# Odd mixer: the output product of six heads inside the last head pair, alpha x in pieces, DVE steps with a PSUM operand

## The chip, the core and the metric

One core of a Trainium2 chip runs the whole kernel, a two-layer diffusion backbone in float32. Five engines with their own instruction queues work on it: TensorE (PE: matmuls and transposes), VectorE (DVE), ScalarE (ACT), GpSimd (POOL), and SyncE (SP), which issues most DMAs. Each queue is worked off in order; an instruction that waits for another engine holds everything behind it on its own engine. The metric is device time in microseconds (us), as the median of several runs.

## What is computed

The part of the reference that the change touches is the odd layer's mixer and the layer norm behind it:

```python
def odd_mixer(h, hc, w_qkv, lam_p, subln_w, w_out, rot, lambda_init, need_ctx):
    ...                                  # q, k, v of 8 heads, rotary on q and k
    k_all = jnp.concatenate([kl, kc], axis=3)      # 512 latent + 256 context tokens
    ob = lax.map(lambda qq: diff_mix(qq, k_all, v_all, lam), qb)
    ...
    def finish(o):
        o = rms_norm(o) * subln_w.astype(f32) * (1.0 - lambda_init)
        return (merge_heads(o).astype(w_out.dtype) @ w_out).astype(h.dtype)

def diff_mix(q, k, v, lam):
    s = jnp.einsum('cbhqd,cbhkd->cbhqk', q, k).astype(jnp.float32) * DIFF_HD ** -0.5
    p = jax.nn.softmax(s, -1)
    a = p[0] - lam * p[1]
    return jnp.einsum('bhqk,bhkd->bhqd', a.astype(v.dtype), v)

x = layer_norm(DEEP_ALPHA * x + g_a * y, ln_g[li, 0], ln_b[li, 0])
hf = modulate(x, sh_f, sc_f)             # input of the FFN
```

The output product is 512 x 1024 by 1024 x 1024: 8 heads of 128 rows, 4 tiles of 128 tokens, and two halves of 512 columns.

## The kernel before

**Numbers in two parts.** Every float32 operand of a large product is split into a high and a low part, and a product is three matmuls (high by high, low by high, high by low). A weight unit is 1024 rows by 256 columns: `unit` (L174) loads it over SP into one of two `raw` buffers (1 MB), GpSimd multiplies it by a gate row where one is given (L185), ACT casts the high part `whi` (L147), and GpSimd or DVE subtracts to get `wlo` (L148). The next load into a `raw` buffer waits until its `wlo` is made.

**Head pairs.** `odd_mixer` works on four pairs of heads. While `attend` works on pair `pr`, head by head and tile by tile, `project(pr + 1)` is put in between step by step: matmuls `opj`, then the rotary steps on DVE (L1576, L1580) with their last sum `otok` on GpSimd (L1582), PE's transposes `oT_ps` of it, and evacuations into `oq` and `ok` on ACT and DVE (L1590 to L1601). A scheduler orders the instructions of each engine by priority.

**One tile of attention.** PE makes the scores `sc`; DVE takes two maxima (L1662), ACT two exponentials (L1665), DVE combines them into `pt` (L1673); PE transposes `pt` into `aT_ps`, ACT and DVE copy it to `aT` (L1681), PE multiplies by v, DVE copies the result into `oall` (L1685), ACT sums its squares (L1686). After four tiles of a head, DVE computes the reciprocal root on 128x4 tiles (`rsqrt`, L127 to L136) and scales `oall` by it and by the subln weight, four steps with two SBUF operands (L1695).

**Output product.** `to_y(h)` transposes a head of `oall` (`yT_ps`) and splits it into `hTh` and `hTl` (L1704, L1705). In the last pair, which has no projection to put in, `sums` fills in the product of heads 0 to 5 for tiles 0 and 1 and the first half of the columns, at a late priority. The rest of the product runs after attention. Units 0 and 1 have no gate; their half of the result is multiplied by the gate on DVE (L1345). Units 2 and 3 are multiplied by the gate on GpSimd. `out_proj_ln` (L1299) then reads x of the layer before, makes alpha x (the normalization's affine part times alpha: product L1323 on DVE, sum L1324 on GpSimd), adds the product (L1346, L1348), normalizes, and makes the FFN's transposed input; the FFN's first matmul is `g_ps`.

Of the kernel before, what the change touches and what calls it, by code (L numbers as in the profile page):

```python
# [97 lines left out]
class Net:  # L98
# [21 lines left out]

    def rsqrt(self, pool, x, n, mul, add, tag):
# [52 lines left out]
    def unit(self, parts, scale=None):  # L174
# [1113 lines left out]
    def out_part(self, accs, units, k, last):  # L1288

        yh, yl = self.hT  # L1290
        for t, ps in accs:
            ts = slice(t * P, (t + 1) * P)
            for u, (wh, wl) in enumerate(units):
                for j, (xi, wi) in enumerate(((yh, wh), (yh, wl), (yl, wh))):
                    self.mm(ps[:, u * 256:(u + 1) * 256], xi[:, k, ts], wi[:, k, :],
                            start=(k == 0 and u == 0 and j == 0), stop=(last and u == 1 and j == 2))

    def out_proj_ln(self, l, w_out, key, src, xh, groups, accp, accs, us, trp, gates=None):

        nc = self.nc  # L1300
        with ExitStack() as st:
            lnp = self.pool(st, f"lnA{l}")
            pp = accp if l == 0 else self.pool(st, f"ps_wout{l}", bufs=2, space=PSUM)
            self.ln_pools(st, f"lnA{l}", trp=trp)
            self.lo_engs = "v"
            self.cparts = 2
            if l == 0:
                self.wps = [self.pool(st, f"wout{l}", bufs=2, side="right")]
                us = [us, [self.unit([w_out[:, u * 256:(u + 1) * 256]]) for u in (2, 3)]]
            if l == 0:  # L1310
                gates = self.gate_rows(lnp, l, 0, 2, self.ln2.tile([P, D], F32, tag="gy", bufs=3, name="gy"))
            else:

                lng, lnb = self.affine_rows(lnp, 0, 1)
                for r in (lng, lnb):
                    nc.scalar.activation(r, r, AF.Copy, scale=ALPHA)

            def load_x(tiles):
                for t in tiles:
                    lx[t] = self.ln2.tile([P, D], F32, tag="lx", bufs=4 if l else 2, name="lx")  # L1320
                    nc.sync.dma_start(out=lx[t], in_=self.x_src(src, t))
                    if l:
                        nc.vector.tensor_mul(lx[t], lx[t], lng)  # L1323
                        nc.gpsimd.tensor_add(lx[t], lx[t], lnb)  # L1324

            lx = {}
            if l:
                load_x((0, 1, 2, 3))
            for grp in groups:
                if l == 0:  # L1330
                    load_x(grp)
# [207 lines left out]
    def odd_mixer(self, acc_st):  # L1539
        nc, a = self.nc, self.a  # L1540
        v, g, s_ = nc.vector, nc.gpsimd, nc.scalar
        with ExitStack() as st0:
            y = self.hT
            pj = self.pool(st0, "ps_opj", bufs=2, space=PSUM)
            with ExitStack() as st:
# [161 lines left out]
                def sums(accs, heads, late=0):  # L1707
                    for h in heads:
                        to_y(h)
                        with self.priority(late):  # L1710
                            self.out_part(accs, us[0], h, h == DHEADS - 1)
# [99 lines left out]
```

## Time and profile before

| what | value |
|---|---|
| median of 3 runs | 2072.14 us (2070.14 to 2078.73) |
| the profiled execution | 2068.32 us |
| its span | 2066.5 us |
| its mean granted TensorE clock | 0.979 |
| PE busy | 1939.9 us (94%) |
| DVE busy | 1231.5 us (60%) |
| GpSimd busy | 775.6 us (38%) |
| ACT busy | 716.3 us (35%) |

The odd mixer takes about 1262 to 1674 us of the span, its last head pair about 1570 to 1628. A busy PE share is counted with matmuls that overlap one another in the pipeline; the distance between the starts of two matmuls in a row is their true price. In square brackets behind a row stands the engine's idle time before it and what ended that time.

### The profile page before, as it was taken

Reading aid. Unit: us, or ns where it says so; the run is one execution under the profiler, and the core shown is the slowest. Engines: PE = TensorE matmul, PEld = TensorE weight load, DVE = VectorE, ACT = ScalarE, POOL = GpSimd, SP = SyncE. Lnnn points to the kernel's source line nnn. Section 1 sums busy time; section 2 is a strip of 40 time slices with the busy share of each in tenths; the row PEclk is TensorE's granted clock in tenths of the full one; section 3 lists DMA queues with packets and bytes.
Section 4 is the critical chain, followed back from the end, with each engine's and each line's share of the span. In section 5 each row is a group of like instructions: output and inputs, shape, how many; then the busy total and the mean of one; then the engine's idle time right before and its main releaser. Section 6 shows DMA issues by size and latency. Waiting matters only on the chain. (4 is left out here: it accounts for less than half of the span.)

```text
span 2066.5 us, 33438 instructions
## 1 busy us (share of the span) xinstructions
PE 1939.9 (94%) x13766; PEld 1666.0 (81%) x13766; DVE 1231.5 (60%) x2423; ACT 716.3 (35%) x1252; POOL 775.6 (38%) x412
## 2 busy tenths in 40 slices
PE   6999999999899999999999998999997989999997
PEld 4777777778888888888888887989896987888886
DVE  2344745444367686666666557356667687756667
ACT  3341343423343432222222225454555343323221
POOL 1233323212322154554554434122213126756572
PEclk8999999999999999999999999999999999999999
DMA  8456344455614321111111112011103143323221
GB/s 261 140 166 178 110 134 141 127 168 169 201 49 156 102 82 62 62 62 62 62 62 62 62 62 90 22 42 42 42 32 95 59 143 102 93 91 102 82 82 41
DMA packets 195585, 201.33 MB, mean 97 GB/s; under 512 B 21112, under 2 KB 183512, under 8 KB 195432
## 3 DMA queue, kind: packets, MB, share of 16 engines
q1 hardware_dynamic: 194136, 197.57, 30.7%
q8 instruction: 108, 1.77, 0.3%
q10 hardware_dynamic: 1296, 1.62, 0.2%
q14 instruction: 45, 0.37, 0.1%
HBM read 185.89 MB, written 13.27 MB: 96 GB/s over the span
## 5 line engine op out<-in xcount | busy, mean ns | idle before, releaser
L148 POOL TENSOR_TENSOR wlo<-raw,whi 128x2048 fp32r<-128x2048 f32 (+2 forms) x154 | 413.6, 2709 | 483.0 <-ACT whi L147 459.7
L1441 DVE SCALAR_TENSOR_TENSOR ac<-g_ps,fconvT,ac 128x441 f32<-128x441 f32 (+2 forms) x352 | 243.8, 694 | 189.0 <-ACT ac L1430 179.3
L147 ACT CAST whi<-raw 128x2048 fp32r<-128x2048 f32 (+2 forms) x177 | 200.3, 1169 | 379.9 <-PE d_ps L115 163.3
L115 PE MATMUL d_ps<-whi,hh 128*128 128x512 f32 x440 | 176.2, 401 | 11.4 <-DVE gt L1390 6.5
L115 PE MATMUL d_ps<-whi,hl 128*128 128x512 f32 x440 | 173.5, 394 | 0.6 <-DVE hl L148 0.6
L115 PE MATMUL d_ps<-wlo,hh 128*128 128x512 f32 x440 | 173.1, 393 | 0.0
L115 PE MATMUL opj<-whi,hTh 128*128 128x256 f32 x512 | 148.1, 289 | 2.1 <-ACT oq L1593 1.6
L115 PE MATMUL g_ps<-hTl,whi 128*128 128x512 f32 (+1 forms) x384 | 145.1, 378 | 3.2 <-POOL hTl L148 3.2
L115 PE MATMUL opj<-whi,hTl 128*128 128x256 f32 x512 | 146.7, 287 | 0.0
L115 PE MATMUL opj<-wlo,hTh 128*128 128x256 f32 x512 | 145.6, 284 | 0.0
L115 PE MATMUL u_ps<-hTh,whi 128*128 128x512 f32 (+1 forms) x384 | 144.6, 377 | 0.0
L115 PE MATMUL u_ps<-hTh,wlo 128*128 128x512 f32 (+1 forms) x384 | 144.6, 377 | 0.0
L115 PE MATMUL g_ps<-hTh,whi 128*128 128x512 f32 (+1 forms) x384 | 144.6, 377 | 0.0
L115 PE MATMUL u_ps<-hTl,whi 128*128 128x512 f32 (+1 forms) x384 | 144.5, 376 | 0.0
L115 PE MATMUL g_ps<-hTh,wlo 128*128 128x512 f32 (+1 forms) x384 | 144.2, 376 | 0.0
L115 PE MATMUL fpj<-whi,hTh 128*128 128x256 f32 x432 | 125.9, 291 | 0.9 <-ACT fo L683 0.9
L115 PE MATMUL fpj<-wlo,hTh 128*128 128x256 f32 x432 | 125.8, 291 | 0.0
L115 PE MATMUL fpj<-whi,hTl 128*128 128x256 f32 x432 | 124.6, 288 | 0.0
L115 PEld LDWEIGHTS d_ps<-whi,hh 128*128 128x128 f32 x440 | 83.3, 189 | 38.9 <-DVE gt L1390 17.2
L115 PEld LDWEIGHTS opj<-whi,hTh 128*128 128x128 f32 x512 | 98.4, 192 | 4.2 <-ACT oq L1593 2.6
L115 PE MATMUL c_ps<-hTh,wlo 128*128 128x256 f32 x352 | 98.9, 281 | 0.0
L115 PE MATMUL c_ps<-hTh,whi 128*128 128x256 f32 x352 | 98.8, 281 | 0.0
(459 smaller groups left out, 4985.2 us busy)
## 6 DMA issues: line engine op xcount, KB each, us to landing
mraw<-in_mod_w_dram SPq DMA_DIRECT2D x80, 512.0 KB
raw<-in_f_w_gate_dram SPq DMA_DIRECT2D x22, 1024.0 KB
raw<-in_f_w_up_dram SPq DMA_DIRECT2D x22, 1024.0 KB
raw<-in_f_w_down_dram SPq DMA_DIRECT2D x22, 1024.0 KB
raw<-in_o_w_qkv_dram SPq DMA_DIRECT2D x12, 1024.0 KB
raw<-in_e_w_in_dram SPq DMA_DIRECT2D x10, 1024.0 KB
mraw<-in_mod_w_dram SPq DMA_DIRECT2D x32, 256.0 KB
raw<-in_e_w_in_dram SPq DMA_DIRECT2D x12, 512.0 KB
```

What stands on the lines that cost most here:

```text
L115: self.nc.tensor.matmul(out, lhsT=lhsT, rhs=rhs, start=start, stop=stop)
L147: self.nc.scalar.copy(h, r)
L148: lo_eng.tensor_sub(l, r, h.bitcast(F32))
L1441: v.scalar_tensor_tensor(out=o, in0=pv[:, r0 + di:r1 + di, c0 + dj:c1 + dj], scalar=cw[(di + 1) * 3 + dj + 1], in1=o, op0=ALU.mult, op1=AL ...
```

## The change

- **Output product.** `early` replaces `sums`: heads 0 to 5 for all four tiles and both halves of the columns (288 matmuls) are filled into the last pair at the late priority, and DVE adds each PSUM result onto alpha x (`rest`). After attention there are heads 6 and 7 (96 matmuls), added by DVE from PSUM, then the normalization in place in `oall`.
- **Weights.** All four units take the gate on GpSimd, and before it a new ACT step multiplies the raw unit by the subln weight, one factor for each partition (`rows`). All four `wlo` are on GpSimd. Unit 0 is loaded in the third pair, unit 1 too in the order that the scheduler makes. The gate comes in two halves (`half_gate`), the first in the third pair.
- **Alpha x.** In the first two pairs `alpha_x(i)` makes alpha x of all rows in 16 pieces of 64 columns: SP reads the piece `xa` (rows of 256 B) and two rows `gb` of the affine part, ACT multiplies `gb` by alpha, GpSimd multiplies and adds (128x256 each), SP writes the piece to `xd[2]`. There is one `xa` and one `gb`. In the last pair the result is read back into `oall` and `rest`.
- **DVE.** `rsqrt_ps` holds y and the sum's addend `zz` in PSUM, so that each step has at most one SBUF operand; the four scalings of `oall` go to ACT.
- `out_proj_ln` now serves layer 0 alone, with the same work as before.

```diff
-    def unit(self, parts, scale=None):
+    def unit(self, parts, scale=None, rows=None):
...
+        if rows is not None:
+            nc.scalar.activation(raw, raw, AF.Copy, scale=rows)
         if scale is not None:
             nc.gpsimd.tensor_mul(rv, rv, scale.unsqueeze(1).to_broadcast([P, KT, 256]))
...
+    def rsqrt_ps(self, pool, hv, y, n, tag):
...
+        v.tensor_scalar(out=y.bitcast(I32), in0=hv.bitcast(I32), scalar1=-0.5, scalar2=MAGIC,
+                        op0=ALU.mult, op1=ALU.add)
+        for i in range(3):
+            v.tensor_mul(w, y, hv)
+            v.tensor_mul(w, y, w)
+            v.scalar_tensor_tensor(out=r if i == 2 else y, in0=w, scalar=1.5, in1=y, op0=ALU.subtract, op1=ALU.mult)
+        return r
...
-                    zz = pb.tile([P, NLT], F32, tag="orz", name="orz")
-                    s_.activation(zz, Zs[:, :, 0], AF.Square, scale=math.sqrt(2 * DH * NORM_EPS))
-                    v.tensor_add(ss, ss, zz)
-                    r = self.rsqrt(pb, ss, NLT, 1.0 / (2 * DH), 0.0, "on")
+                    zz, yy = (ps[:, 3 * P + i * NLT:3 * P + (i + 1) * NLT] for i in range(2))
...
+                    r = self.rsqrt_ps(pb, ss, yy, NLT, "on")
                     for t in range(NLT):
-                        v.scalar_tensor_tensor(out=oall[:, t, hc], in0=oall[:, t, hc], scalar=r[:, t:t + 1], in1=sub,
-                                               op0=ALU.mult, op1=ALU.mult)
+                        s_.activation(oall[:, t, hc], oall[:, t, hc], AF.Copy, scale=r[:, t:t + 1])
...
+                def early(heads):
+
+                    for n in range(2):
+                        for t in range(NLT):
+                            ps = pj.tile([P, 512], F32, tag="wo", name="wo_ps")
+                            with self.priority(LATE):
+                                for h in heads:
+                                    self.out_part([(t, ps)], us[n], h, h == heads[-1])
+                                    if h == heads[len(heads) // 2 - 1]:
+                                        yield
+                                for o, c0, n_ in rest(t, n):
+                                    v.tensor_add(o, ps[:, c0:c0 + n_], o)
+                            yield
...
+                def out_unit():
+                    sl = slice(len(us) * 256, (len(us) + 1) * 256)
+                    us.append(self.unit([w_out[:, sl]], gates[len(us) // 2][:, (len(us) % 2) * 256:][:, :256],
+                                        sub[:, 0:1]))
...
+                def alpha_x(i):
+
+                    cs = slice(i * 64, (i + 1) * 64)
+                    nc.sync.dma_start(out=xa, in_=self.xd[1][:LAT, cs].rearrange("(t p) n -> p t n", p=P))
+                    for j, n in enumerate(("ln_g", "ln_b")):
+                        nc.sync.dma_start(out=gb[:, j], in_=a[n][0, 1, cs].partition_broadcast(P))
+                    s_.activation(gb, gb, AF.Copy, scale=ALPHA)
+                    for j, op in enumerate((g.tensor_mul, g.tensor_add)):
+                        op(xa, xa, gb[:, j].unsqueeze(1).to_broadcast([P, NLT, 64]))
+                    nc.sync.dma_start(out=self.xd[2][:LAT, cs].rearrange("(t p) n -> p t n", p=P), in_=xa)
...
                         for _ in attend(2 * pr + i, cur["q"], cur["k"], cur["v"], i):
                             with self.priority(100 if pr < 3 else 0):
-                                for _ in range(3 if pr < 3 else 1):
+                                for _ in range(3 if pr < 3 else 2):
                                     next(fill, None)
+                            done += 1
+                            if pr < 2:
+                                alpha_x(8 * pr + done - 1)
+                            if pr == 2 and done == 6:
+                                out_unit()
                     for _ in fill:
                         pass
+                for h in (6, 7):
+                    to_y(h)
```

How the change moves instructions, at three places.

GpSimd, first head pair, around the rotary sums `otok` of the second pair's k and q. Before:

```order
L1582 TENSOR_TENSOR otok_12500<-otok_12500,ob_12501 128x512
L1582 TENSOR_TENSOR otok_12564<-otok_12564,ob_12565 128x512
L1582 TENSOR_TENSOR otok_12738<-otok_12738,ob_12739 128x512
L1582 TENSOR_TENSOR otok_12802<-otok_12802,ob_12803 128x512
L148 TENSOR_TENSOR wlo_13197<-raw_13194,whi_13196 128x2048
```

After (a piece is two steps on `xa`):

```order
L1748 TENSOR_TENSOR xa_12884<-xa_12884,gb_12883 128x256 x2
L1574 TENSOR_TENSOR otok_12500<-otok_12500,ob_12501 128x512
L1748 TENSOR_TENSOR xa_12884<-xa_12884,gb_12883 128x256 x2
L1574 TENSOR_TENSOR otok_12564<-otok_12564,ob_12565 128x512
L1748 TENSOR_TENSOR xa_12884<-xa_12884,gb_12883 128x256 x6
L1574 TENSOR_TENSOR otok_12738<-otok_12738,ob_12739 128x512
L1748 TENSOR_TENSOR xa_12884<-xa_12884,gb_12883 128x256 x2
L1574 TENSOR_TENSOR otok_12802<-otok_12802,ob_12803 128x512
```

One piece now stands ahead of the first sum, one ahead of the second, three ahead of the third and one ahead of the fourth.

GpSimd from the third pair's last projection weights to the end of the mixer. Before (`raw_15500`, `raw_15507` are units 2 and 3; units 0 and 1 are split on DVE):

```order
L148 TENSOR_TENSOR wlo_15126<-raw_15123,whi_15125 128x2048
L1582 TENSOR_TENSOR otok_14988<-otok_14988,ob_14989 128x512
L1582 TENSOR_TENSOR otok_15117<-otok_15117,ob_15118 128x512
L1197 TENSOR_TENSOR gate0_15494<-gate0_15494,raw_15492 128x1024
L185 TENSOR_TENSOR raw_15500<-raw_15500,gate0_15494 128x2048
L185 TENSOR_TENSOR raw_15507<-raw_15507,gate0_15494 128x2048
L148 TENSOR_TENSOR wlo_15504<-raw_15500,whi_15503 128x2048
L148 TENSOR_TENSOR wlo_15511<-raw_15507,whi_15510 128x2048
```

After (`raw_15640` is unit 1, `raw_15659` unit 2, `raw_15667` unit 3; unit 0, `raw_15482`, took its gate earlier):

```order
L161 TENSOR_TENSOR wlo_15234<-raw_15231,whi_15233 128x2048
L202 TENSOR_TENSOR raw_15640<-raw_15640,gate0_14715 128x2048
L1574 TENSOR_TENSOR otok_15099<-otok_15099,ob_15100 128x512
L161 TENSOR_TENSOR wlo_15487<-raw_15482,whi_15486 128x2048
L1574 TENSOR_TENSOR otok_15225<-otok_15225,ob_15226 128x512
L161 TENSOR_TENSOR wlo_15645<-raw_15640,whi_15644 128x2048
L1737 TENSOR_TENSOR gate1_15636<-gate1_15636,rest_15635 128x512
L202 TENSOR_TENSOR raw_15659<-raw_15659,gate1_15636 128x2048
L202 TENSOR_TENSOR raw_15667<-raw_15667,gate1_15636 128x2048
L161 TENSOR_TENSOR wlo_15664<-raw_15659,whi_15663 128x2048
L161 TENSOR_TENSOR wlo_15672<-raw_15667,whi_15671 128x2048
```

Unit 1's product with the gate now stands ahead of the third rotary sum of the last pair's projection, and the `wlo` of units 0 and 1 and a second gate sum ahead of the products of units 2 and 3.

ACT at the start of the last pair. Before (`aT_15539`, `aT_15598` are its first two tiles, `raw_15500` and `raw_15507` units 2 and 3):

```order
L1681 COPY aT_15539<-aT_ps_15540 128x512
L1665 ACTIVATE sc_15578,oZ_15517<-sc_15578,mx_15591 128x768
L1704 CAST hTh_68<-yT_ps_15558 128x512
L1686 ACTIVATE pt_15530,oss_15516<-oall_12879 128x128
L147 CAST whi_15503<-raw_15500 128x2048
L1665 ACTIVATE pt_15648,oZ_15517<-sc_15636,mx_15646 128x768
L147 CAST whi_15510<-raw_15507 128x2048
L1681 COPY aT_15598<-aT_ps_15599 128x512
```

After (`aT_15698`, `aT_15776` are the first two tiles, `raw_15659` and `raw_15667` units 2 and 3):

```order
L200 ACTIVATE raw_15667<-raw_15667,sub_12366 128x2048
L1695 CAST hTh_68<-yT_ps_15604 128x512
L160 CAST whi_15663<-raw_15659 128x2048
L1687 ACTIVATE oall_12876<-oall_12876,rs_y_15573 128x128 x4
L1695 CAST hTh_68<-yT_ps_15611 128x512
L1695 CAST hTh_68<-yT_ps_15618 128x512
L160 CAST whi_15671<-raw_15667 128x2048
L1695 CAST hTh_68<-yT_ps_15625 128x512
L1673 COPY aT_15698<-aT_ps_15699 128x512
L1657 ACTIVATE sc_15834,oZ_15676<-sc_15834,mx_15847 128x768
L1673 COPY aT_15776<-aT_ps_15777 128x512
```

The casts of units 2 and 3 stood between the first and the second tile's `aT` copies; now they and a scaling stand ahead of the first, and the second follows it.

## Rows read from the trace of the kernel before

**Rows 1.** by stretch: busy us (instructions) of PE, PEld, DVE, ACT, POOL; PEclk; DMA

```profile
1262.00:1560.00 298.00, 283.47 (x2203) 268.34 (x2202) 171.91 (x355) 145.15 (x277) 70.58 (x30) 0.98 0.14 45
1580.00:1590.00 10.00, 3.17 (x15) 3.17 (x16) 7.97 (x10) 4.72 (x6) 6.57 (x2) 0.67 0.00 1
1590.00:1627.00 37.00, 33.00 (x246) 29.91 (x246) 27.53 (x63) 20.31 (x49) 6.64 (x2) 1.00 0.23 72
```

**Rows 2.** PE's own timeline: start, us, line, operation [idle before <-releaser]

```profile
1586.83 0.58 PE L115 MATMUL wo_ps<-whi,hTl 128*128 128x256 f32 x1 [7.62 <-DVE hTl L1705]
...
1588.48 0.41 PE L115 MATMUL wo_ps<-whi,hTl 128*128 128x256 f32 x1
...
1626.05 1.58 PE L115 MATMUL aT_ps<-ov,aT 128*128 128x128 f32 x12
1627.38 0.37 PE L115 MATMUL wo_ps<-whi,hTl 128*128 128x256 f32 x1
...
1635.24 0.28 PE L115 MATMUL wo_ps<-whi,hTl 128*128 128x256 f32 x1
...
1658.81 0.58 PE L115 MATMUL wo_ps<-whi,hTh 128*128 128x256 f32 x1 [5.18 <-DVE lx L1348]
...
1674.46 0.28 PE L115 MATMUL g_ps<-hTh,whi 128*128 128x256 f32 x1
```

**Rows 3.** DVE's timeline early in the last pair and at attention's end

```profile
1575.80 3.88 DVE L136 SCALAR_TENSOR_TENSOR rs_y<-rs_w,rs_y 128x4 f32<-128x4 f32 x1
1579.72 5.33 DVE L1695 SCALAR_TENSOR_TENSOR oall<-oall,rs_y,sub 128x128 f32<-128x128 f32 x4
...
1630.80 1.14 DVE L1695 SCALAR_TENSOR_TENSOR oall<-oall,rs_y,sub 128x128 f32<-128x128 f32 x4
```

**Rows 4.** DVE's groups by line over 1262 to 1700 us: busy us, mean ns

```profile
L1673 DVE SCALAR_TENSOR_TENSOR pt<-sc,nl,pt 128x768 f32<-128x768 f32 x32 | 32.5, 1016 | 0.8
...
L1695 DVE SCALAR_TENSOR_TENSOR oall<-oall,rs_y,sub 128x128 f32<-128x128 f32 x32 | 13.3, 476 | 0.2
```

**Rows 5.** GpSimd's timeline

```profile
1291.31 1.27 POOL L1582 TENSOR_TENSOR otok<-otok,ob 128x512 f32<-128x512 f32 x1 [4.85 <-DVE ob L1580]
1309.02 1.28 POOL L1582 TENSOR_TENSOR otok<-otok,ob 128x512 f32<-128x512 f32 x1 [16.44 <-DVE ob L1580]
...
1343.62 1.29 POOL L1582 TENSOR_TENSOR otok<-otok,ob 128x512 f32<-128x512 f32 x1 [15.89 <-DVE ob L1580]
...
1517.71 4.61 POOL L148 TENSOR_TENSOR wlo<-raw,whi 128x2048 fp32r<-128x2048 f32 x1
1526.53 1.29 POOL L1582 TENSOR_TENSOR otok<-otok,ob 128x512 f32<-128x512 f32 x1 [4.21 <-DVE rs_y L128]
...
1575.13 8.99 POOL L185 TENSOR_TENSOR raw<-raw,gate 128x2048 f32<-128x2048 f32 x2 [11.71 <-DVE rs_w L135]
```

**Rows 6.** PE's timeline behind a rotary sum of GpSimd

```profile
1527.87 0.66 PE L119 MATMUL oT_ps<-ident,otok 128*128 128x128 f32 x4 [0.22 <-POOL otok L1582]
```

**Rows 7.** SP's queue: the DMAs it issues, by time of issue

```profile
257.22 0.34 SPq L859 DMA_DIRECT2D gdr<-G  x1
...
259.02 3.26 SPq L862 DMA_DIRECT2D XZ<-gdr  x7
...
536.87 0.36 SPq L1063 DMA_DIRECT2D gt<-zd  x1
...
1522.35 0.37 SPq L181 DMA_DIRECT2D raw<-in_o_w_out_dram  x1
```

**Rows 8.** where two of those transfers end: GpSimd's timeline, then DMA by stretch

```profile
540.65 1.84 POOL L1064 TENSOR_TENSOR o_dn<-o_dn,gt 128x768 f32<-128x768 f32 x1 [2.00 <-DMA gt<-zd]
...
1526.00:1527.00 1.00, 1.00 (x11) 1.00 (x10) 0.93 (x5) 0.00 (x0) 0.47 (x1) 1.00 0.77 264
```

**Rows 9.** ACT's timeline at the start of the last pair

```profile
1564.68 1.91 ACT L147 CAST whi<-raw 128x2048 fp32r<-128x2048 f32 x1 [1.55 <-issue]
...
1590.06 0.58 ACT L1681 COPY aT<-aT_ps 128x512 f32<-128x512 f32 x1
```

More of the change, by code (lines that the diff above doesn't have):

```diff
@@ L1285, in h_tiles, with out_part @@
             self.split(hf, self.hT[0][:, ks, sl], self.hT[1][:, ks, sl], nc.gpsimd if kq % 2 else nc.vector)
-    def out_part(self, accs, units, k, last):
+    def out_part(self, accs, units, k, last, first=0):
         yh, yl = self.hT
@@ L1318, in load_x @@
[L1318 to L1328, printed above, removed]
+            self.wps = [self.pool(st, "wout0", bufs=2, side="right")]
@@ L1705, in to_y @@
                     v.tensor_sub(y[1][:, h, :LAT], ps, yh.bitcast(F32))
[L1707 to L1711, printed above, removed]
-                        yield
+                def early(heads):
[10 more added lines that the diff above has]
+                            yield
                 nxt = {}
@@ L1747, in odd_mixer @@
                     for _ in fill:
                         pass
+                for h in (6, 7):
+                    to_y(h)
+                acc = [oall[:, t, :] for t in range(NLT)]
                 sts.close()
[L1750 to L1756 removed]
@@ L1757, in odd_mixer @@
-                accs += more
-                for _ in sums(accs, (7,)):
-                    pass
-                stb.close()
-                acc = self.acc_tiles(acc_st, 1, NLT, side="right")
-                self.out_proj_ln(1, w_out, "f1", 2, acc, ((0, 1), (2, 3)), pj, dict(accs), us, trp, [gate])
+                stb.close()
+                self.ln_pools(st, "lnA1", trp=trp)
+                po = self.pool(st, "ps_wout1", bufs=4, space=PSUM)
+                self.lo_engs = "v"
+                self.cparts = 2
@@ new lines, in odd_mixer @@
+                for grp in ((0, 1), (2, 3)):
+                    sts = {t: self.ln_stats() for t in grp}
+                    for t in grp:
+                        for n in range(2):
+                            ps = po.tile([P, 512], F32, tag="wo", name="wo_ps")
+                            for h in (6, 7):
+                                self.out_part([(t, ps)], us[n], h, h == 7, first=6)
+                            for o, c0, n_ in rest(t, n):
+                                v.tensor_add(acc[t][:, n * 512 + c0:n * 512 + c0 + n_], ps[:, c0:c0 + n_], o)
+                            self.ln_half(acc[t], sts[t], n)
+                        self.ln_tile(acc[t], sts[t], acc[t], None)
+                    with self.priority(100):
+                        self.h_tiles("f1", grp, [acc[t] for t in grp])
```

105 lines of the change are left out of this document (55 added, 50 removed).

## The prediction

> **What bounds the kernel now.** I read first the busy time by stretch. Over the first three head pairs of the odd mixer TensorE (PE) is busy 283.5 of 298 us, and both later stretches that the change rewrites have holes [rows 1]: at 1580 to 1590 us, early in the last pair, PE works 3.2 of 10 us at a granted clock of 0.67, and from 1590 to 1627, the rest of that pair, 33.0 of 37. Then PE's own timeline says what ended each hole [rows 2]: 7.62 us behind hTl, a subtraction of DVE, at 1586.83, and 5.18 us behind lx, a sum of DVE, at 1658.81. After the first hole the next matmuls come at 0.21 us each instead of 0.12 (8 of them between 1586.83 and 1588.48), so a hole costs about 1 us more than its length. Last, DVE and GpSimd side by side: while GpSimd multiplies two weight units by the gate (8.99 us from 1575.13) [rows 5], DVE's step on four columns takes 3.88 us, and four scalings take 5.33 us where the same four take 1.14 later [rows 3]. So in that hole DVE does not lack input; its steps on two SBUF operands stand still. The step pt of line 1673, with one operand in PSUM, has a mean of 1016 ns over 32 executions, while line 1695, on SBUF alone, has 476 ns where four in a row take 1.14 us [rows 3, 4].
>
> **1. The tail.** From the end of the last PV product (1626.05 + 1.58 = 1627.6) to the FFN's first g_ps at 1674.46 is 46.8 us [rows 2]. By the order, 308 of the output product's 384 matmuls are left there, and the second hole lies among them. The changed program has 204 left there: 108 of heads 0 to 5 that the late priority pushed back, and 96 of heads 6 and 7. At the pitch of the 67 matmuls from 1627.38 to 1635.24, 0.117 us [rows 2], that is 23.9 us. Twenty transposes stand between them before g_ps, 2.4 us at the same pitch (an estimate). What waits there: head 7's transposes need its rsqrt and scaling, which end at 1630.80 + 1.14 = 1631.9, 4.3 us after the last PV [rows 3]; about 33 matmuls (3.9 us) stand ahead of them, so with the scaling on ACT I add 1 us. The normalization of tiles 0 and 1 lies under the matmuls of tiles 2 and 3. Sum 27.3 us: **-19.5 us**, from -21 (no wait) to -14.5 (5 us of normalization uncovered, as long as the hole there now).
>
> **2. Start of the last pair.** The steps that stood still go: zz, y and the sum of rsqrt now have a PSUM operand, the scaling is on ACT. But all four weight units now take the gate on GpSimd, and ACT's order puts both casts of units 2 and 3 ahead of the first aT copy of this pair. The chain: unit 1's cast ends at 1564.68 + 1.91 = 1566.6 [rows 9], its wlo on GpSimd takes 4.6 more [rows 5]: 1571.2. This frees the buffer of unit 3, whose load takes about 4.6 us (issued at 1522.35, bytes still moving from 1526 to 1527 [rows 7, 8]): 1575.8. The gate row and its bias are queued behind it on SP, another 2 to 3 us (estimate: each is a quarter of the bytes): 1578.5. Gate sum 0.65 (half of 1.28), two products at 4.5, one cast 1.9: 1590.1. Before, at 1590.06 the second tile's aT is copied [rows 9]; the first tile waits in the new order too, but both are then copied in a row. So the same progress at the same time: the hole has another cause, same size. **0 us**, from -3 (gate row lands beside the load) to +3.
>
> **3. The rest of the last pair.** By the order 180 product matmuls now stand before the last PV, 42 of them in the hole; before, 76, some 10 of them up to the hole's end. That is (138 - 66) x 0.117 = 8.4 us more; 20 transposes of yT move into the hole (-2.4), and PE's 4.0 idle us [rows 1] can take some. **+3 us**, from +2 (all idle time filled) to +6 (none).
>
> **4. Unit 1 ahead of a rotary sum.** Its load is issued at 1522.35, when wlo of 1517.71 has freed the buffer [rows 5, 7], and lands at about 1527.0. New on ACT is its scaling by subln (128x2048, taken as the cast of that size, 1.9 us [rows 9]), which stands ahead of Square, the oall scalings and the q evacuations: to 1528.9. Behind it comes the product with the gate on GpSimd, 4.5 us [rows 5]: 1533.4; and only behind that, in GpSimd's order, the rotary sum that now runs at 1526.53, 1.29 us: 1534.7. PE's transposes follow that sum with 0.22 us of idle time at 1527.87 [rows 6], so they have no slack. **+6.5 us**, from +2 (other PE work stands in the gap) to +9; and +1 for the clock after such a hole, by the first one. The scalings of units 0, 2 and 3 are on ACT too, whose busy share in the three pairs is 145 of 298 us [rows 1]: +1, from 0 to 2.
>
> **5. Alpha x in 16 pieces.** One buffer, so each piece is read, GpSimd's two steps, write, and only then the next read. Read: between 1.8 us (a small transfer, 257.22 to 259.02) and 3.8 us (gt, 512 B rows, 536.87 to 540.65) [rows 7, 8]. GpSimd: two steps of 128x256, half a 128x512 (1.28 [rows 5]) each, 1.3. Write: 1.8 to 3.8 by the same rows. A cycle is 4.9 to 8.9 us; I take 6.7, nearer to the small transfer, since a piece has a third of gt's bytes. Three pieces stand on GpSimd between the rotary sums of 1291.31 and 1309.02: 16.4 us are free there, three cycles need 20.1, so the third sum is 3.7 us late, and PE's transposes behind it. Of the next five pieces, up to the sum at 1343.62 [rows 5]: 1312.7 + 1.3 + 33.5 = 1347.5 against 1347.3. **+4 us**, from 0 (cycle of 5.5 or less) to +10 within my range. No row here shows a transfer in rows of 256 B beside such work, so both ends stay open. The Trainium skill, DMA: Bandwidth & Descriptors, section Specifications, asks for at least 512 B for line rate and tells of a read-modify-write below that, which speaks against these pieces; by it read and write would sit at their long ends, which is rival (b), and no row here tests it. The SP queue's weight loads stand behind pieces, but each is issued tens of us before its cast.
>
> **6. The first three pairs otherwise.** Line 1695 costs 13.3 us where 32 x 0.285 = 9.1 would do [rows 3, 4]; this and the rsqrt steps leave DVE, mostly off PE's path: **-1.5 us**, 0 to -3.
>
> **Sum:** -19.5 + 0 + 3 + 6.5 + 1 + 1 + 4 - 1.5 = -5.5 us. The profiled execution took 2068.3 us (span 2066.5), 3.8 under the median 2072.1; the difference goes on the median: 2066.6.
>
> **Rivals.** (a) The waits of 4 and 5 stay short: cycle of 5.5 us, other work of PE under unit 1's chain (+2), and 2 and 3 as above: -19.5 + 3 + 2 + 1 - 1.5 = -15, and to -23 at the low ends: 2049 to 2058. For it: GpSimd is busy only 70.6 of 298 us in these pairs [rows 1], so lateness can be made up between two sums; against: 0.22 us of idle time before 1527.87, on PE's side [rows 6]. 0.28. (b) Slower: the pieces' cycle. At 7.6 us the two late sums add 6.4 + 4.7 = 11 us, which eats the forecast's gain (-9.5 without term 5); at 8.7 they add 9.7 + 10.2 = 20: +10, 2082.5. That is the point from which it is measurably slower; at 8.9 us, 2084. For it: 256 B rows, two more broadcasts per piece in the same queue; against: a small transfer takes 1.8 us. 0.13. (c) A PSUM operand does not spare DVE GpSimd's products: the held steps (about 8 us [rows 3]) return behind the chain of 2: 2074. Against: the mean of line 1673 [rows 4]. 0.08. The Trainium skill, GPSIMD Engine Reference, section 1 (Specifications), names as contenders with GpSimd DVE instructions in a two-port mode or with two SBUF inputs; by that (c) would not come, and the trace agrees with 1016 ns in line 1673. (d) The product's matmuls lengthen the last pair one for one and the tail's normalization is uncovered: -14.5 + 6 + 8.5 + 4 - 1.5 = +2.5: 2075. 0.06. The forecast has the remaining 0.45.
>
> **Numbers.** Half a per cent, 10.4 us, is about what a measurement of this kernel can tell from no change. Faster than 2061.8: (a) and a quarter of the forecast's own spread, 0.40. Slower than 2082.5: (b) and the upper ends together, 0.13. Between: 0.47. The likeliest is the sum, 2066.5; the range goes from the low ends (2049) to 2083, where (b) begins.
>
> **What would show it.** Term 1: g_ps starts about 27 us after the last PV, no hole behind DVE. Term 2: no DVE step of four columns over 0.3 us while GpSimd multiplies, but aT copies of two tiles in a row behind whi. Term 4: a hole of 5 to 7 us in PE near the third pair's sixth tile, its rotary sum behind raw<-raw,gate. Term 5: pieces 6 to 7 us apart, the third rotary sum of the first pair directly behind one. The forecast is wrong if PE shows no hole at unit 1, if pieces come every 5 or every 8.5 us, or if the last pair grows by over 6 us.

## The result, and the profile after

The changed kernel takes 2083.73 us (median of 10 runs, 2077.07 to 2095.27) beside 2070.16 us (10 runs, 2066.32 to 2078.73) for the kernel before: a ratio of 1.0062, 95% interval 1.0045 to 1.0079. It is slower by 13.6 us; the prediction was 2066.5, in a range of 2049 to 2083.

Single executions scatter, and part of that scatter lies ahead of the odd mixer. The first step of its input normalization (`ln_ps`, which waits 3.54 to 3.58 us for ACT's `acc` in every profile of this study) starts at 1272.35 us in the profile of before, at 1275.07 in that of after, and between 1271.85 and 1283.88 in the others, though no kernel changes anything ahead of it. The latest start, in e8, goes with a mean granted clock of 0.94 in the first 500 us; in e7, the earliest, it is 0.97. So the stages below are counted from that row, the entry. PV is the product of a tile of attention with v, `aT_ps<-ov,aT`; there are 32, eight to a head pair. The 20th falls where the third rotary sum of the last pair's projection is due.

| stage (us, from the profiles) | before | after | e1 | e2 | e3 | e4 | e5 | e6 | e7 | e8 | e9 | e10 |
|---|---|---|---|---|---|---|---|---|---|---|---|---|
| entry to first PV | 58.3 | 65.4 | 59.4 | 65.4 | 64.9 | 58.3 | 58.3 | 60.9 | 62.0 | 61.4 | 60.8 | 61.3 |
| entry to 20th PV | 250.5 | 259.1 | 246.9 | 261.0 | 259.3 | 248.5 | 243.8 | 254.1 | 255.0 | 250.0 | 255.1 | 256.8 |
| 20th to 24th PV | 44.3 | 56.3 | 56.2 | 42.7 | 42.7 | 46.8 | 42.3 | 42.6 | 42.6 | 44.4 | 56.7 | 42.7 |
| 24th to last PV (last pair) | 58.9 | 67.2 | 68.7 | 68.3 | 59.9 | 61.3 | 58.1 | 58.7 | 58.7 | 65.2 | 68.9 | 58.7 |
| last PV to first g_ps | 48.5 | 29.2 | 29.2 | 29.0 | 27.9 | 48.2 | 48.4 | 27.9 | 30.8 | 30.7 | 29.1 | 30.7 |
| first g_ps to the span's end | 392.0 | 396.7 | 396.9 | 397.0 | 397.4 | 392.1 | 391.1 | 397.2 | 390.4 | 390.5 | 397.3 | 390.6 |

The span grows by 17.1 us, from 2066.5 to 2083.6: 2.7 ahead of the entry, 8.7 up to the 20th PV, 12.0 in the third pair's last tiles, 8.3 in the last pair, -19.3 in the tail, and 4.7 given back in the FFN.

PE's own timeline after: start, us, operation, and in brackets the idle time before it and what ended that. [rows 2] and [rows 6] show the same places before.

```profile
1291.48 0.66 PE L119 MATMUL oT_ps<-ident,otok 128*128 128x128 f32 x4 [3.33 <-POOL otok L1574]
...
1318.88 0.66 PE L119 MATMUL oT_ps<-ident,otok 128*128 128x128 f32 x4 [2.79 <-POOL otok L1574]
...
1546.78 1.11 PE L119 MATMUL oT_ps<-ident,otok 128*128 128x128 f32 x4 [7.18 <-POOL otok L1574]
...
1549.18 0.41 PE L115 MATMUL opj<-whi,hTh 128*128 128x256 f32 x1
1549.39 0.41 PE L115 MATMUL opj<-wlo,hTh 128*128 128x256 f32 x1
...
1602.35 0.39 PE L115 MATMUL wo_ps<-whi,hTh 128*128 128x256 f32 x1 [3.09 <-ACT hTh L1695]
...
1611.14 0.58 PE L115 MATMUL wo_ps<-whi,hTh 128*128 128x256 f32 x1 [3.92 <-ACT hTh L1695]
...
1657.71 1.58 PE L115 MATMUL aT_ps<-ov,aT 128*128 128x128 f32 x12
...
1686.86 0.39 PE L115 MATMUL g_ps<-hTh,whi 128*128 128x256 f32 x1
...
1752.57 0.80 PE L115 MATMUL d_ps<-whi,hh 128*128 128x512 f32 x1 [7.25 <-DVE oall L1479]
```

Read down: the two holes of [rows 2] behind DVE are gone, and no wait of 5 us stands between the last PV and g_ps. In the mixer other waits took their place, the larger ones behind GpSimd's `otok` or ACT's `hTh`. Behind the hole of 7.18 us matmuls start 0.21 us apart; the stretch shows why in its granted clock, which is 0.50, the lower of its two levels, from 1546.8 to 1552.1 us (columns: busy us of PE, PEld, DVE, ACT, POOL with instructions, granted clock, DMA share, GB/s):

```profile
1546.00:1556.00 10.00, 7.71 (x39) 7.15 (x40) 5.09 (x9) 6.17 (x9) 1.19 (x2) 0.69 0.00 0
...
1600.00:1627.00 27.00, 18.10 (x107) 17.22 (x108) 8.84 (x20) 13.65 (x23) 19.34 (x5) 0.81 0.44 152
```

GpSimd's timeline after, where [rows 5] had little but rotary sums:

```profile
1302.54 1.55 POOL L1748 TENSOR_TENSOR xa<-xa,gb 128x256 f32<-128x256 f32 x2 [4.32 <-ACT gb L1746]
1309.03 1.54 POOL L1748 TENSOR_TENSOR xa<-xa,gb 128x256 f32<-128x256 f32 x2 [4.94 <-DMA xa<-xd]
1316.09 1.52 POOL L1748 TENSOR_TENSOR xa<-xa,gb 128x256 f32<-128x256 f32 x2 [5.51 <-DMA xa<-xd]
1317.57 1.26 POOL L1574 TENSOR_TENSOR otok<-otok,ob 128x512 f32<-128x512 f32 x1
...
1541.01 4.50 POOL L202 TENSOR_TENSOR raw<-raw,gate 128x2048 f32<-128x2048 f32 x1 [7.33 <-ACT raw L200]
1545.46 1.26 POOL L1574 TENSOR_TENSOR otok<-otok,ob 128x512 f32<-128x512 f32 x1
...
1601.59 1.27 POOL L1737 TENSOR_TENSOR gate<-gate,rest 128x512 f32<-128x512 f32 x1 [6.99 <-DMA rest<-in_mod_b_dram]
1602.94 9.04 POOL L202 TENSOR_TENSOR raw<-raw,gate 128x2048 f32<-128x2048 f32 x2
```

Two rotary sums start the moment the step ahead of them ends, at 1317.57 and 1545.46: DVE's `ob` for them had ended at 1314.60 and 1537.62, so they were ready and stood in the queue. The last two rows are the second half of the gate and the products of units 2 and 3.

ACT's timeline after ([rows 9] is its part of the last pair before):

```profile
1404.14 0.31 ACT L1746 ACTIVATE gb<-gb 128x128 f32<-128x128 f32 x1 [3.56 <-DMA gb<-in_ln_b_dram]
...
1538.92 2.00 ACT L200 ACTIVATE raw<-raw,sub 128x2048 f32<-128x2048 f32 x1 [5.54 <-DMA raw<-in_o_w_out_dram]
...
1607.53 1.90 ACT L160 CAST whi<-raw 128x2048 fp32r<-128x2048 f32 x1 [5.23 <-POOL raw L202]
...
1612.02 1.90 ACT L160 CAST whi<-raw 128x2048 fp32r<-128x2048 f32 x1 [0.45 <-POOL raw L202]
...
1614.53 0.58 ACT L1673 COPY aT<-aT_ps 128x512 f32<-128x512 f32 x1
...
1617.81 0.58 ACT L1673 COPY aT<-aT_ps 128x512 f32<-128x512 f32 x1 [1.80 <-PE aT_ps L119]
```

In each of the first three rows ACT itself stands still for a load or for GpSimd, with attention's steps queued behind it. ACT's waits by cause from 1270 to 1630 us (us in total, times, longest) show that it is no single case:

```profile
ACT gb L1746 <- DMA gb<-in_ln_b_dram: 29.5, 11, 5.7
ACT raw L200 <- DMA raw<-in_o_w_out_dram: 9.2, 3, 5.5
ACT whi L160 <- POOL raw L202: 5.7, 2, 5.2
```

DVE's timeline after, the answer to [rows 3], and one step of the FFN:

```profile
1286.99 0.69 DVE L1568 TENSOR_TENSOR otok<-opj,ca 128x512 f32<-128x512 f32 x1 [4.01 <-DMA ca<-in_cattn_dram]
...
1602.94 0.15 DVE L130 TENSOR_TENSOR rs_w<-aT_ps,rs_w 128x4 f32<-128x4 f32 x1
...
1604.53 0.15 DVE L131 SCALAR_TENSOR_TENSOR rs_y<-rs_w,aT_ps 128x4 f32<-128x4 f32 x1
...
1744.22 4.84 DVE L161 TENSOR_TENSOR hl<-ac,hh 128x512 fp32r<-128x512 f32 x1
```

The second and third row run under GpSimd's product of 1602.94 and take 0.15 us; the step of [rows 3] took 3.88.

### The profile page after: what moved, and what is told of

It reads as the page before. It is cut to its first block, busy times and chain, and to the rows that moved or that the text cites. A ratio compares the mean times of both kernels' runs of the same rounds, so it can differ in the third digit from the quotient of the medians.

```text
span 2083.6 us, 33657 instructions
## 1 busy us (share of the span) xinstructions
PE 1945.2 (93%) x13766; PEld 1670.9 (80%) x13766; DVE 1198.1 (58%) x2389; ACT 733.6 (35%) x1302; POOL 806.6 (39%) x446
## 4 chain that ended last, share of the span: by engine, by line
PE 50%; DVE 10%; DMA 4%; POOL 4%; issue 4%; ACT 4%; SPq 0%; POOLq 0%; DVEq 0%; ACTq 0%
PE u_ps L115 11%; PE d_ps L115 11%; PE g_ps L115 10%; PE c_ps L115 6%; PE opj L115 3%; PE wo_ps L115 3%; PE aT_ps L115 1%; PE fpj L115 1%; PE sc L115 1%; DMA xd<-xa 1%; DVE gt L1381 1%; DVE hl L161 1%; POOL wlo L161 1%; DMA xa<-xd 1%; POOL xa L1748 1%
## 5 line engine op out<-in xcount | busy, mean ns | idle before, releaser
L161 POOL TENSOR_TENSOR wlo<-raw,whi 128x2048 fp32r<-128x2048 f32 (+2 forms) x156 | 423.1, 2735 | 493.3 <-ACT whi L160 431.8
L1432 DVE SCALAR_TENSOR_TENSOR ac<-g_ps,fconvT,ac 128x441 f32<-128x441 f32 (+2 forms) x352 | 243.8, 694 | 189.1 <-ACT ac L1421 179.3
L115 PEld LDWEIGHTS d_ps<-whi,hh 128*128 128x128 f32 x440 | 83.1, 189 | 41.6 <-DVE gt L1381 17.1
L115 PEld LDWEIGHTS opj<-wlo,hTh 128*128 128x128 f32 x512 | 100.1, 195 | 0.0
L115 PEld LDWEIGHTS opj<-whi,hTl 128*128 128x128 f32 x512 | 99.6, 195 | 0.1
```

Source lines behind the costliest of these rows:

```text
L115: self.nc.tensor.matmul(out, lhsT=lhsT, rhs=rhs, start=start, stop=stop)
L161: lo_eng.tensor_sub(l, r, h.bitcast(F32))
L1432: v.scalar_tensor_tensor(out=o, in0=pv[:, r0 + di:r1 + di, c0 + dj:c1 + dj], scalar=cw[(di + 1) * 3 + dj + 1], in1=o, op0=ALU.mult, op1=AL ...
```

## The experiments

All times are medians; a ratio is to the kernel before in the same session, with its 95% interval. Runs of different sessions are compared best by their ratios, since the median of the kernel before goes from 2069.80 to 2073.66 us between sessions. Line numbers in rows of an experiment are its own.

**e1: no alpha pieces.** What do the pieces cost in all?

```diff
-                            if pr < 2:
-                                alpha_x(8 * pr + done - 1)
...
-                                nc.sync.dma_start(out=o, in_=self.x_src(3, t)[:, c0:c0 + o.shape[1]])
+                                nc.sync.dma_start(out=o, in_=self.x_src(2, t)[:, c0:c0 + o.shape[1]])
```

> The changed kernel without the 16 pieces of alpha x (reads, ACT and GpSimd steps and writes are left out; the last pair reads the plain x, so this part of the computation is missing). Theory: the pieces stand ahead of rotary sums on GpSimd and cost 8.5 us by the lag of PV products between 1262 and 1534 us, so this run is 8 to 10 us under the changed kernel (about 2074), and PE's transposes again follow their rotary sums by the times of the kernel before. Rival (traffic): the pieces only take DMA and GpSimd time that nobody waits for, and the lag is the layer's weights arriving late: then within 2 us of the changed kernel.

Measured: 2073.91 us, ratio 1.0019 (1.0006 to 1.0031), 9.8 us under the changed kernel (8.9 by the two ratios); the stage up to the 20th PV shrinks by 12.2 us and the others stay within 1.5. Unit 1's hole is as before:

```profile
1534.57 1.11 PE L119 MATMUL oT_ps<-ident,otok 128*128 128x128 f32 x4 [7.48 <-POOL otok L1574]
```

So the pieces cost 9 to 12 us, about the upper end of term 5, and have no part in the other losses.

**e2: unit 1 later.** Units 1 to 3 take their factor from a copy that DVE makes out of the last pair's finished q, so ACT's scaling and GpSimd's product of unit 1 can't be ordered ahead of the rotary sum. Such an artificial dependency is called an edge below.

```diff
+                        v.scalar_tensor_tensor(out=sub2, in0=cur["q"][3][:, 1, LAT - 1:LAT].bitcast(F32), scalar=0.0,
+                                               in1=sub, op0=ALU.mult, op1=ALU.add)
...
-                                        sub[:, 0:1]))
+                                        (sub if len(us) == 0 else sub2)[:, 0:1]))
```

> The changed kernel with one edit: the subln factor of units 1 to 3 is copied by a step that reads the last evacuated q columns, so unit 1's scaling and its product with the gate come behind the third pair's rotary sums. Theory: the hole of 7.18 us at unit 1 goes with its half clock and the ACT wait: 10 to 12 us less than the changed kernel (about 2072). Rival: the work is only moved, and the same 8 us of ACT and GpSimd time come back as a later start of the last pair: 0 to 4 us less.

Measured: 2079.01 us, ratio 1.0032 (1.0014 to 1.0049). The stage from the 20th to the 24th PV falls from 56.3 to 42.7 us, under the 44.3 of before, and the sum has no wait ahead of PE:

```profile
1539.14 0.66 PE L119 MATMUL oT_ps<-ident,otok 128*128 128x128 f32 x4 [0.21 <-POOL otok L1574]
```

The place and the mechanism of the hole are shown. The time is a miss: the median gains 4.7 us (6.2 by the two ratios), where 10 to 12 was expected and the rival had 0 to 4, while this one profile's stage gains 13.6. The profiled execution is the fastest of the seven and has the highest mean granted clock (0.978; the others 0.971 to 0.976); what the slower ones lost is not shown.

**e3: heads of the queues.** e2, and two more steps that waited at the head of a queue in the last pair: the gate's second half reuses the first half's tile and is loaded earlier, with its bias in the idle `xa`, and unit 3 is loaded and scaled after the pair's first tile.

```diff
-                    t = pool.tile([P, 512], F32, name=f"gate{n}")
+                    t = pool.tile([P, 512], F32, name=f"gate{n}") if n == 0 else gates[0]
...
+                            if pr == 3 and done == 1:
+                                v.scalar_tensor_tensor(out=sub2, in0=oall[:, 0, 6 * P:6 * P + 1], scalar=0.0, in1=sub,
+                                                       op0=ALU.mult, op1=ALU.add)
+                                out_unit()
```

> As the run before, and two more edits: the second half of the gate takes the place of the first as soon as unit 1 has its product (no wait for the last pair's memory), and unit 3 takes its factor only after the last pair's first tile, so its cast stands behind that tile's aT copy. The pieces of alpha x stay. Theory: the start of the last pair loses its holes (3.09 and 3.92 us and the clock after them) too: 16 to 20 us less than the changed kernel, 2064 to 2068, 0 to 6 us less than the kernel before. Rival: the last pair is bound by its own attention and product work on PE, and only the 10 to 12 us of unit 1 go: 2072.

Measured: 2064.63 us, ratio 0.9969 (0.9948 to 0.9990), 14.4 us under e2, faster than before. The last pair falls from 68.3 to 59.9 us. ACT copies `aT` ahead of the casts:

```profile
1571.97 0.59 ACT L1673 COPY aT<-aT_ps 128x512 f32<-128x512 f32 x1 [2.31 <-PE aT_ps L119]
1577.92 1.90 ACT L160 CAST whi<-raw 128x2048 fp32r<-128x2048 f32 x1
1579.73 0.58 ACT L1673 COPY aT<-aT_ps 128x512 f32<-128x512 f32 x1
1581.97 1.91 ACT L160 CAST whi<-raw 128x2048 fp32r<-128x2048 f32 x1
```

**e4: the DVE part alone.** The kernel before with `rsqrt_ps`, `oall` scaled on ACT, and the subln weight moved into ACT's scaling of the units.

```diff
-                    r = self.rsqrt(pb, ss, NLT, 1.0 / (2 * DH), 0.0, "on")
+                    r = self.rsqrt_ps(pb, ss, yy, NLT, "on")
...
+            nc.scalar.activation(raw, raw, AF.Copy, scale=rows)
```

> The kernel before with one part of the change: rsqrt with y and the addend in PSUM, the four scalings on ACT, subln as an ACT step on each weight unit; no pieces, no moved product. Theory: DVE's steps no longer stand still while GpSimd multiplies units 2 and 3, the hole of 7.62 us and its half clock go, the new ACT steps of 2.0 us each take 2 to 4 us back: 4 to 7 us less than the kernel before (2063 to 2066). Rival: a PSUM operand does not spare DVE, or another wait takes the hole's place: within 2 us of the kernel before.

Measured: 2076.65 us, ratio 1.0014 (1.0000 to 1.0029): a miss: not faster, and if anything a little slower. ACT now waits for the units' loads (first two rows), and the hole of [rows 2] is longer, with another name at its end:

```profile
1495.95 2.00 ACT L198 ACTIVATE raw<-raw,sub 128x2048 f32<-128x2048 f32 x1 [3.72 <-DMA raw<-in_o_w_out_dram]
...
1531.68 2.01 ACT L198 ACTIVATE raw<-raw,sub 128x2048 f32<-128x2048 f32 x1 [6.04 <-DMA raw<-in_o_w_out_dram]
```

```profile
1596.04 0.58 PE L115 MATMUL wo_ps<-whi,hTh 128*128 128x256 f32 x1 [9.41 <-ACT hTh L1718]
```

**e5: the same without the subln weight.** ACT's step on the units is left out, and with it that factor of the result.

```diff
-            nc.scalar.activation(raw, raw, AF.Copy, scale=rows)
```

> The DVE part alone again, now without the ACT steps that multiply the weight units by subln (that factor is left out of the computation). The run with them came out 5.7 us above the kernel before, with ACT waiting 3.7 and 6.0 us for the loads of units 0 and 1 and PE a hole of 9.4 us behind a cast of hTh. Theory: the two waits for loads go (about 7 us of lag), and the hole in the last pair stays at 6 to 8 us, because ACT's casts of units 2 and 3, which wait for GpSimd's two products, stand in its queue ahead of the evacuations; so 2 to 4 us under the kernel before (2067 to 2069): DVE standing still was only one of two waits of the same length. Rival: with DVE free the hole goes, 8 to 10 us under the kernel before (2061 to 2063).

Measured: 2064.66 us, ratio 0.9971 (0.9960 to 0.9983). By the two ratios the step on the units cost e4 about 9 us, more than the DVE steps gain. The hole stays:

```profile
1584.41 0.58 PE L115 MATMUL wo_ps<-whi,hTh 128*128 128x256 f32 x1 [7.02 <-ACT hTh L1718]
```

```profile
1581.97 1.90 ACT L160 CAST whi<-raw 128x2048 fp32r<-128x2048 f32 x1 [2.27 <-POOL raw L200]
1583.78 0.58 ACT L1718 CAST hTh<-yT_ps 128x512 fp32r<-128x512 f32 x1
```

The held DVE steps and the casts behind GpSimd's products were two waits that ended at about the same time; taking one away shows the other. Most of the gain lies elsewhere: the stage up to the 20th PV is 6.7 us shorter than before.

**e6: paced pieces.** e3, with alpha for each piece written by DVE out of the tile just finished, so that piece i can't be scaled before tile i is done.

```diff
+                    v.tensor_scalar(out=alph, in0=oall[:, t_, hd_ * P:hd_ * P + 1], scalar1=0.0, scalar2=ALPHA,
+                                    op0=ALU.mult, op1=ALU.add)
...
-                    s_.activation(gb, gb, AF.Copy, scale=ALPHA)
+                    s_.activation(gb, gb, AF.Copy, scale=alph[:, 0:1])
```

> The three edits of e3_queue_heads, and the 16 pieces of alpha x paced: the alpha factor of a piece is written by a one-column DVE step that reads the tile of attention just finished, so a piece can't stand on GpSimd before that. Same pieces, same bytes. Theory: the price of the pieces is their place ahead of rotary sums (12 us of lag against the run without them), not their work: 7 to 11 us under e3_queue_heads, 2054 to 2058. Rival: it is their traffic and the GpSimd and ACT time: within 3 us of e3_queue_heads (2062 to 2066), with the lag now spread over the second and third pair.

Measured: 2061.18 us, ratio 0.9958 (0.9942 to 0.9973). That is 3.5 us under e3 by the medians and 2.3 by the two ratios, whose intervals overlap, so the time alone doesn't tell e6 from e3, and the rival (within 3 us) is not excluded. In the profiles the stage up to the 20th PV is 5.2 us shorter. ACT's waits for `gb` fall from 32.9 us in e3 to 4.9:

```profile
ACT gb L1749 <- DMA gb<-in_ln_b_dram: 4.9, 3, 2.1
```

By that stage not quite half of the pieces' 12.2 us is gone, which is less than the theory expected.

**e7: normalization first.** e6, with the last normalization's transposed tiles (`h_tiles`) at normal priority instead of a late one.

```diff
-                    with self.priority(100):
-                        self.h_tiles("f1", grp, [acc[t] for t in grp])
+                    self.h_tiles("f1", grp, [acc[t] for t in grp])
```

> As e6_paced, with the transposes and evacuations of the normalized tiles at the end of the mixer at normal priority instead of 100 later, so that PE takes those of tiles 0 and 1 between the product's matmuls and starts the FFN with g_ps alone. In the changed kernel and its variants the FFN gives back 4.7 to 5.4 us behind the first g_ps. Theory: that loss is the normalization of tiles 2 and 3 left uncovered and the first conv steps that start late behind mixed g_ps and u_ps; it shrinks to 0 to 2 us, so 2 to 4 us under e6_paced. Rival: it comes from DVE's held step behind GpSimd's products in the FFN, whatever stands before it: within 1.5 us of e6_paced.

Measured: 2058.30 us, ratio 0.9938 (0.9922 to 0.9953), 11.5 us under before in the same session and the lowest ratio here (its interval overlaps those of e6, e8 and e10). g_ps starts 2.9 us later behind the last PV, and the FFN behind it is 6.8 us shorter:

```profile
1718.20 0.79 PE L115 MATMUL d_ps<-whi,hh 128*128 128x512 f32 x1 [4.12 <-DVE oall L1479]
```

The wait that was 7.25 us after the change is 4.12. The FFN stage is as short in e8 and e10, which have the same edit.

**e8: unit 0 later too.** e7 with an edge from the third pair's sixth tile for unit 0, as units 1 to 3 have one.

```diff
+                                v.scalar_tensor_tensor(out=sub1, in0=oall[:, 1, 5 * P:5 * P + 1], scalar=0.0, in1=sub,
+                                                       op0=ALU.mult, op1=ALU.add)
...
-                                        (sub if len(us) == 0 else sub2)[:, 0:1]))
+                                        (sub1 if len(us) == 0 else sub2)[:, 0:1]))
```

> The version of e7 with one more edge: unit 0's factor column is copied by a VectorE step that reads an output of the third pair, as units 1 to 3 already read one of the last pair, so that ScalarE's scaling and GpSimd's gate product of unit 0 stand behind that pair's early steps instead of ahead of them in the in-order queues. Theory (a ScalarE or GpSimd step on a late load holds the queue behind it): the stage up to the 20th PV group gets 4 to 6 us shorter than in e7 (254.95), and the time is 2052 to 2055. Rival (what is left in that stage is the pieces' own cycle, and unit 0's steps lie beside it): stage and time stay within 1.5 us of e7, 2057 to 2060. If unit 0's steps only move their wait into the third pair's end, the 20th to 24th PV stage (42.6) grows by what the first stage loses, and the time is that of e7 too.

Measured: 2063.52 us, ratio 0.9946 (0.9925 to 0.9967): not faster than e7. The first stage does shrink by 5.0 us, and 1.8 and 6.5 come back in the next two:

```profile
1588.35 0.58 PE L115 MATMUL wo_ps<-wlo,hTh 128*128 128x256 f32 x1 [5.08 <-POOL wlo L161]
```

```profile
1577.12 0.72 POOL L1737 TENSOR_TENSOR gate<-gate,xa 128x256 f32<-128x256 f32 x1
1583.10 0.73 POOL L1737 TENSOR_TENSOR gate<-gate,xa 128x256 f32<-128x256 f32 x1 [5.26 <-PE yT_ps L119]
1583.78 4.51 POOL L161 TENSOR_TENSOR wlo<-raw,whi 128x2048 fp32r<-128x2048 f32 x1
```

The second `gate` sum needs its bias row, which SP issues at 1577.87 when the first sum has freed `xa`, 0.7 us behind the load of a unit. The row names a transpose of PE that ends at about the same time; that the bias came last is inferred. `wlo` stands behind it on GpSimd though its cast ended at 1580.43, and PE waits for `wlo`. The edge is too late a one: it moved the wait instead of removing it.

**e9: gb scaled on GpSimd.** The changed kernel; only this step moves from ACT.

```diff
-                    s_.activation(gb, gb, AF.Copy, scale=ALPHA)
+                    g.tensor_scalar(out=gb, in0=gb, scalar1=ALPHA, scalar2=None, op0=ALU.mult)
```

> The changed kernel with one step of each alpha piece moved: the multiplication of gb by alpha is on GpSimd instead of ScalarE; reads, writes, GpSimd's two steps and the order stay. In the changed kernel ScalarE waits 29.5 us in 11 of these 16 steps for gb's load (5.7 at most), with exponentials queued behind. Theory (a good half of the pieces' 12 us in the stage up to the 20th PV group comes from ScalarE held at the head of its queue, the rest from GpSimd's late rotary sums): the stage shrinks from 259.1 to 251 to 254, the sums of the first pair stay late, and the time is 2076 to 2079. Rival (it is GpSimd's lateness alone, ScalarE's waits lie beside other work): stage and time stay within 2 us of the changed kernel, or get worse by the GpSimd steps added.

Measured: 2085.54 us, ratio 1.0061 (1.0038 to 1.0084): no gain. The first PV comes 4.6 us earlier behind the entry and the 20th 4.0, since ACT no longer waits for `gb`; GpSimd does, 41.8 us in 13 times from 1270 to 1440 us, and a later rotary sum is late instead:

```profile
1375.16 0.95 PE L119 MATMUL oT_ps<-ident,otok 128*128 128x128 f32 x4 [4.03 <-POOL otok L1574]
```

PE's waits from the entry to the 20th PV tell the two ways apart. After the change they are:

```profile
PE oT_ps L119 <- POOL otok L1574: 6.9, 5, 3.3
PE aT_ps L119 <- DVE pt L1665: 3.9, 5, 1.5
PE aT_ps L115 <- ACT aT L1673: 2.9, 2, 1.6
```

The first comes by GpSimd's late sums, the other two by ACT's late exponentials and copies: 6.9 and 6.8 us, where e1 without the pieces has 3.6 and 1.1. In e9 they are 8.3 and 2.5. So ACT's wait was the larger part of what PE lost to the pieces here; taking it off ACT gives back 4.0 us of the stage, part of it returns behind the sums, and the time shows no gain.

**e10: the same in e7.** The same line, with `alph[:, 0:1]` as the factor.

> e7 with the same move: alpha's multiplication of gb on GpSimd instead of ScalarE. In e7 ScalarE waits 5.8 us in 3 of these steps. Theory: a gain of 1 to 3 us over e7 in the stage up to the 20th PV group (254.95), time 2055 to 2058. Rival: paced pieces no longer hold anything, and moving their ScalarE step changes nothing (within 1 us), or GpSimd's rotary sums come later instead.

Measured: 2059.18 us, ratio 0.9944 (0.9922 to 0.9967): that of e7. The stage up to the 20th PV is 1.8 us longer, as the rival had it.

## Why the prediction was wrong

**What bounds the kernel** was half right. DVE's steps on two SBUF operands did stand still: under the same product they now take 0.15 us instead of 3.88 [rows 3]. The Trainium skill, GPSIMD Engine Reference, section 1 (Specifications), names DVE instructions in a two-port mode or with two SBUF inputs as those that contend with GpSimd; these rows agree, and rival (c) fell. But e5 shows that they were not the only cause of the hole.

**Term 1, the tail: right at its place, cut short at its end.** -19.5 was forecast to g_ps, -19.3 came. The step that failed is that the sum ended at g_ps. The FFN gave back 4.7 us: its first convolution step on DVE runs 19.1 us behind the first g_ps instead of 15.9, and PE's wait for the first d_ps is 7.25 us where it was 4.52 before:

```profile
1735.14 0.80 PE L115 MATMUL d_ps<-whi,hh 128*128 128x512 f32 x1 [4.52 <-DVE acc L1488]
```

In e7, with `h_tiles` at normal priority, the give-back is gone. The net -14.6 is the short end of the term's range.

**Term 2, the last pair's start: chain right, 5.2 us lost.** From the end of unit 1's cast (1589.92) to that of the last cast (1613.92) are 24.0 us; the working had 23.5. The step that failed is "both are then copied in a row": the second copy comes 3.3 us after the first, since an exponential of ACT (1615.01) and PE's transposes for that tile still had to run, and PE ran at a clock of 0.81. Before, the first tile had gone ahead of the hole. The 26th PV is thus 5.2 us later behind the 24th, where 0 (-3 to +3) stood. PE's idle time between the two even fell, from 10.9 to 7.3 us: it has 137 matmuls and transposes there instead of 72, the moved work, and runs much of it at the lower clock.

**Term 3, the rest of that pair:** +3 forecast, +3.1 measured from the 26th to the last PV.

**Term 4, unit 1: right in kind, too small.** The hole is 7.18 us where 6.5 was forecast, behind exactly the queue that was named. Two smaller waits of PE follow, 1.52 us for DVE's `pt` at 1555.73 and 1.88 for ACT's `oq` at 1567.79, ahead of which ACT scales unit 2. In all PE is idle for 11.3 us of this stage, where it was for 2.1 before. For the clock after the hole +1 was forecast; PE runs at 0.50 for 5.3 us behind it, which costs about half of that, 2.7 (an estimate; a shorter stretch at the lower level came in this stage before and after alike). The 9.2 us of added idle time and 2.7 make 11.9 of the stage's 12.0. The failing step: the clock was taken too small, and only the first hole was priced, not the waits that follow it.

**Terms 5 and 6, the first pairs: the largest miss.** +4 - 1.5 was forecast, +8.7 came. Both terms were sized wrong, in opposite directions: e1 puts the pieces at 12.2 us up to the 20th PV, three times the 4 of term 5, and e5 puts the DVE steps at -6.7, not -1.5. The two make +5.5. The remaining 3.2 us were not tested in the changed kernel; unit 0's steps, which term 4 had as a part of +1, can account for them, since e8 takes 5.0 us out of this stage by moving these. Their cycle was chosen well, 6.5 and 7.1 us between the rows of 1302.54, 1309.03 and 1316.09 (6.7 in the working). The parts, from SP's queue:

```profile
1306.60 0.38 SPq L1743 DMA_DIRECT2D xa<-xd  x1
...
1310.60 0.38 SPq L1749 DMA_DIRECT2D xd<-xa  x1
...
1313.07 0.38 SPq L1743 DMA_DIRECT2D xa<-xd  x1
```

The read issued at 1306.60 ends GpSimd's wait at 1309.03, 2.4 us later; the write of 1310.60 lets the next read go after 2.5 us; that read takes 3.0. The Trainium skill, DMA: Bandwidth & Descriptors, section Specifications, asks for at least 512 B for line rate; the transfers lie between the ends of 1.8 and 3.8 us, not at the long one, and rival (b) did not come in its form. What failed is the list of instructions. The working costed the pieces' DMAs and GpSimd steps against GpSimd's two late sums, and not the ACT step `gb`, which waits for a load at the head of ACT's queue: 29.5 us in 11 of 16 times, exponentials behind it. By PE's waits under e9 this is the larger part of what the pieces cost PE up to the 20th PV. Behind the row of 1404.14 PE then waits too, 0.65 us for ACT's exponential at 1405.87 and 1.12 for `pt` at 1408.31. Nor did it see that four loads (`xa`, two of `gb`, the gate row) are now issued ahead of the rotary constants `ca`, and the first sum is late already: DVE waits 4.01 us for `ca` at 1286.99. Most of that is not the piece's. In e1, without its three loads but with the first gate half's, the wait is still there:

```profile
1285.62 0.69 DVE L1568 TENSOR_TENSOR otok<-opj,ca 128x512 f32<-128x512 f32 x1 [2.91 <-DMA ca<-in_cattn_dram]
```

In e4 and e5, with neither, the same step waits 1.62 us for PE and not for `ca`, as before. The third sum lies 42.5 us behind the entry instead of 36.7, half of that from the second sum already.

**The sum.** Corrected: 2.7 (ahead of the mixer) + 8.7 + 12.0 + 8.3 - 14.6 = +17.1 in the profiles, 13.6 in the medians. The outcome was none of the rivals; it had the price of (b) by another way. The terms' own upper ends add up to +16.5, about what came, but the range stopped at 2083, and being slower got a chance of 0.13. That holds if the terms miss independently; three of them share one mechanism and missed together.

**That mechanism** is told by the runs together: a step that waits for a load or for GpSimd, put ahead of attention's steps on an in-order queue. Moving three such steps in e2 and e3 returns 19.1 us of the median. Pacing another one takes 5.2 us off its stage, of which the time shows 2 to 3, not clear of noise, and with the normalization put first the change as a whole is worth -11.5 us in e7. Open are the 7 us of the pieces' cost that pacing leaves in the stage, and the part of e2's gain that its median doesn't show.

## What to carry to other kernels

For each step that a change adds, ask on every engine what it waits for and what is queued behind it; a free engine share says nothing of that, and a wait at the head of ACT's queue can reach PE in full: ACT's 5.54 us for unit 1's load stand in the chain of PE's hole of 7.18, while 29.5 us of waits for `gb` cost PE only a part of that. Work that is filled in early needs an edge that holds it back, made out of data that is ready at the right time; an edge that is too late moves the wait to the next place, as e8 did. Follow a saving past the end of its stage, and when two waits end together, expect the first repair to show the second.

## What the runs showed of the hardware

A DVE step on 128x4 with one operand in PSUM takes 0.15 us in the middle of GpSimd's 9 us product, where the two-SBUF step had taken 3.88. The FFN's `hl`, still with two SBUF operands, shows the other side: 4.84 us at 1744.22, beside a subtraction of GpSimd, where the same step takes 0.69 at 1757.61. After its hole of 7.18 us PE was granted a clock of 0.50 for 5.3 us. A transfer of 128 KB in rows of 256 B takes 2.4 to 3.0 us to its reader. And the same instructions ahead of the mixer end anywhere from 1271.85 to 1283.88 us, the latest with the lowest clock in the first 500 us (0.94 against 0.95 to 0.97), so a difference of a few us between two profiles is worth nothing without a common row to count from.
